# Comparing against an index row that lies in PSUM: one operand moved in the gates' one-hot matrices

## The chip, the cores and the metric

The kernel runs on one core of one Trainium2 chip. The metric is the device time of one execution in microseconds (us), the median of several runs; less is better. PE is the engine of the matmuls, DVE the vector engine, ACT the engine of activations, POOL the third elementwise engine, and SP issues most of the DMAs. SBUF is the working memory; PSUM is the memory into which matmuls write, eight banks of 512 fp32 numbers in each of 128 partitions.

## What is computed

A network of three blocks over 256 tokens of width 1024. The change lies in the first block's last part, a mixture of 16384 experts of one neuron each (PEER). Every token picks 16 experts for each of 8 heads, by the 16 best of 16 x 16 sums of two top-16 lists over 128 keys each. An expert's number is `i1 * 128 + i2`, and its weight is a softmax over the 16 best scores.

```python
def peer_ffn(h, w_query, sub_keys1, sub_keys2, expert_u, expert_v):
    ...
    e_idx = (jnp.take_along_axis(i1, top_p // PEER_TOPK, axis=-1) * PEER_N_KEYS
             + jnp.take_along_axis(i2, top_p % PEER_TOPK, axis=-1))
    gate = jax.nn.softmax(top_s, axis=-1)
    ...
    def block(args):
        xc, ic, gc = args
        u = jnp.take(expert_u, ic, axis=0)
        act = jax.nn.gelu(jnp.einsum('cd,ced->ce', xc, u).astype(jnp.float32), approximate=False)
        vv = jnp.take(expert_v, ic, axis=0)
        return jnp.einsum('ce,ced->cd', (gc * act).astype(vv.dtype), vv)
```

## The kernel before

The kernel gathers nothing. It computes all 16384 experts for all 256 tokens and multiplies each by its gate, which is zero for those not picked. `peer` (line 1026) does this in three stages.

First the queries, their scores and the two top-16 lists; `gates(t)` (line 1120) leaves, for each token, 128 picks in `pick`: index 0 is the one key's number, index 1 the other's, index 2 the weight. A pick is a partition there, a token a column.

Second, a loop over 128 tiles of 128 experts. `products(j)` (line 1195) multiplies tile j of `peer_u` with the tokens: 24 matmuls of 128x128 by 128x256 (eight pieces of the width, each as three products of split numbers, lines 106 to 108) into one PSUM bank, and ACT applies GELU. `prepare(j + 3)` readies a later tile: four DMAs from SP (`fetch`, line 1176), a DVE transpose into `uT`, and two halves of splitting, ACT for `uh` and POOL for `ul`.

Beside this loop, `spread` (line 1142) builds the gates, in 64 steps of N = 4 tokens. For a token, a one-hot matrix `b` says which pick has which first key, and `g` the same for the second key, scaled by the weight; the product of both, a 128x128 matmul, sums the weights of the picks into a table of gates. The function `ones(t0)` (line 1144) makes the matrices of four tokens: two DVE comparisons over 128x512 (`is_equal` of the index row `i128`, repeated for each token, with `pick`, repeated along the row), then four ACT scalings. The profile names them `one`. Then come four products (line 1158, eight matmul records, since fp32 goes in two passes) into one PSUM bank. Where the activations of a tile of experts are there already, DVE multiplies them with the gates in place (`G<-G,g`); where not, ACT copies the gates (`G<-g`), and `products` multiplies later (`G<-y,G`). `G` is read and written there in strides of 1 KB.

Third, the gated activations are multiplied with `peer_v` (lines 1281 to 1307).

Order: `V`, `A` and `P` (line 1033) keep DVE, ACT and POOL instructions of this function in the order of the program. PE's order is set by the planner of the framework. `advance` (line 1220) says how many steps of `spread` go with each tile; `ones` of the next step is issued after the products of this one.

PSUM is one pool (line 39) with three tags: "g" of four banks, "o" of two, "y" of two. `psum` (line 60) takes one of "g"; `pw` (line 64) goes in a cycle of three calls, g, g, o, with `k.turn` as its counter for the whole kernel. Within the second stage, the products take "g", GELU's results "y", and the spread products whatever `pw` gives. After the loop, line 1275 takes both "o" and both "y".

Of the kernel before, what the change touches and what calls it, by code (L numbers as in the profile page):

```python
# [11 lines left out]
F = mybir.dt.float32  # L12
# [1013 lines left out]
def peer(k, then):  # L1026


    nc, a, tc = k.nc, k.a, k.tc
# [3 lines left out]
    V, A, P = (Ordered(tc, e) for e in (nc.vector, nc.scalar, nc.gpsimd))  # L1033
    with ExitStack() as es:
# [8 lines left out]
        gap(k, part, GAPS["query"])  # L1043
        e1 = ExitStack()
        pool = e1.enter_context(tc.tile_pool(reuse_waits="tile", name="pu", bufs=1, side="right"))
        i128 = pool.tile([128, 128], F, name="i128")
        nc.gpsimd.iota(i128, pattern=[[1, 128]], base=0, channel_multiplier=0, allow_small_or_imprecise_dtypes=True)

        ph, pl = (pool.tile([128, 8, T], FR, name=x) for x in ("ph", "pl"))
        pick = pool.tile([128, 3, T], F, name="pick")  # L1050
# [6 lines left out]
        for i, nm in enumerate(("peer_sub_keys1", "peer_sub_keys2")):  # L1057
            skn = arena.tile([128, 128], F, name="skn", bufs=2)
            nc.scalar.dma_start(skn, a[nm][0])
            p = k.psum([128, 128])  # L1060
# [79 lines left out]
        N = 4  # L1140

        def spread(pool, first):

            def ones(t0):
                b, g = (pool.tile([128, N, 128], F, name=f"one{i}", bufs=2) for i in range(2))
                for o, i in ((b, 0), (g, 1)):
                    V.tensor_tensor(o, i128[:, None, :].to_broadcast([128, N, 128]),
                                    pick[:, i, t0:t0 + N, None].to_broadcast([128, N, 128]), op=OP.is_equal)
                for t in range(N):
                    A.activation(g[:, t], g[:, t], AF.Copy, scale=pick[:, 2, t0 + t:t0 + t + 1])  # L1150
                return b, g
            nxt = ones(0)
            yield 1
            for t0 in range(0, T, N):
                b, g = nxt
                p = k.pw([128, N, 128])
                for t in range(N):
                    nc.tensor.matmul(p[:, t], g[:, t], b[:, t], start=True, stop=True)
                if t0 + N < T:
                    nxt = ones(t0 + N)  # L1160
                n = state["done"]
                for x, at in ((G[0], 0), (G[1], NA)):
                    x = x[:, :, t0:t0 + N].rearrange("p j t -> p t j")
                    to = at + x.shape[2]
                    c = min(max(n, at), to)
                    if c > at:
                        V.tensor_tensor(x[:, :, :c - at], x[:, :, :c - at], p[:, :, at:c], op=OP.mult)
                    if c < to:
                        A.activation(x[:, :, c - at:], p[:, :, c:to], AF.Copy)
                state["built"] = t0 + N  # L1170
                yield (NB - 3 - first) * N / T
# [91 lines left out]
        for j in range(NB):  # L1263
            if not side and not state["built"]:
                e2.close()
                ow = e2.enter_context(tc.tile_pool(reuse_waits="tile", name="po", bufs=1, side="right"))
                side.append(spread(ow, j))
                pace = 1
            products(j)
# [4 lines left out]
        pool = es.enter_context(tc.tile_pool(reuse_waits="tile", name="pv", bufs=1))  # L1274
# [24 lines left out]
        for i in range(NB):  # L1299
# [3 lines left out]
            for c in range(8):  # L1303
                o, s = yp[c // 2][:, c % 2], slice(c * 128, c * 128 + 128)
# [734 lines left out]
@with_exitstack  # L2039
def program(ctx, tc, a, out, dbg=None, parts=None):  # L2040
    k = K(ctx, tc, a, out, dbg)
    first_half(k)
    norm = lambda l, j: lambda: Norm(k, k.of_norm(l, j), by4=l == j == 1)
    peer(k, norm(0, 0))
    with tc.tile_pool(reuse_waits="tile", name="ev", bufs=1) as pool:
        E = Even(pool)
        k.beside = even_weights(k, E, pool, 0)
        ffn(k, 0, 0, norm(0, 1))
        for _ in k.beside:
            pass  # L2050
        even_mixer(k, 0, E, norm(0, 2))
    with tc.tile_pool(reuse_waits="tile", name="s5", bufs=1) as ps5:
        S = S5(ps5)
        with tc.tile_pool(reuse_waits="tile", name="s5t", bufs=1) as tmp:
            k.beside = (None for _ in s5_weights(k, S, tmp, 0) for _ in range(2))
            ffn(k, 0, 1, norm(1, 0))
            ffn(k, 1, 0, norm(1, 1))
            for _ in k.beside:
                pass
        odd_mixer(k, 1, S, norm(1, 2))  # L2060
    ffn(k, 1, 1, lambda: Last(k))
    k.norm.done()
# [47 lines left out]
```

## Time and profile before

| | us |
|---|---|
| timed runs, median of 3 | 2390.65 |
| lowest and highest | 2383.12, 2391.75 |
| the profiled execution | 2374.76 |
| its span, first to last instruction | 2372.7 |
| PE busy | 2219.6 (94%) |
| DVE busy | 1801.2 (76%) |
| ACT busy | 1275.3 (54%) |
| POOL busy | 853.1 (36%) |
| mean granted TensorE clock | 0.964 |

The busy shares are means over stages with different limits. PE's busy time counts matmuls that overlap, so 94% isn't PE at its peak. [...] The profile names an instruction by what it writes and reads (`one<-i,pick` writes a `one` from `i128` and `pick`), leaving out the numbers of buffers. Lines 1001 are those of a helper, through which all DVE, ACT and POOL instructions of `peer` that keep their order are issued.

### The profile page before, as it was taken

Reading aid. Unit: us, or ns where it says so; the run is one execution under the profiler, and the core shown is the slowest. Engines: PE = TensorE matmul, PEld = TensorE weight load, DVE = VectorE, ACT = ScalarE, POOL = GpSimd, SP = SyncE. Lnnn points to the kernel's source line nnn. Section 1 sums busy time; section 2 is a strip of 40 time slices with the busy share of each in tenths; the row PEclk is TensorE's granted clock in tenths of the full one; section 3 lists DMA queues with packets and bytes.
Section 4 is the critical chain, followed back from the end, with each engine's and each line's share of the span. In section 5 each row is a group of like instructions: output and inputs, shape, how many; then the busy total and the mean of one; then the engine's idle time right before and its main releaser. Section 6 shows DMA issues by size and latency. Waiting matters only on the chain.

```text
span 2372.7 us, 46823 instructions
## 1 busy us (share of the span) xinstructions
PE 2219.6 (94%) x17962; PEld 2096.6 (88%) x17962; DVE 1801.2 (76%) x3277; ACT 1275.3 (54%) x2691; POOL 853.1 (36%) x829
## 2 busy tenths in 40 slices
PE   7999998788799999899999999999999999989998
PEld 4877687788799998899999899987999999979998
DVE  7888786898778999677777666667876666687664
ACT  4543433734478776455555554446656666536444
POOL 2132220678778787444444200100352221141000
PEclk8999798899999999999999999999999999989999
DMA  7522123446555554455555576521655455515663
GB/s 263 160 90 81 45 72 96 121 116 152 152 133 144 136 149 123 148 194 195 196 196 196 169 224 192 166 81 46 192 181 186 153 178 186 187 50 169 204 202 119
DMA packets 299232, 358.38 MB, mean 151 GB/s; under 512 B 19324, under 2 KB 271680, under 8 KB 297984
## 3 DMA queue, kind: packets, MB, share of 16 engines
q1 hardware_dynamic: 290432, 349.52, 47.6%
q10 hardware_dynamic: 8032, 5.54, 0.8%
q8 instruction: 141, 2.31, 0.4%
q14 instruction: 83, 0.68, 0.1%
q0 software_dynamic: 544, 0.33, 0.1%
HBM read 354.28 MB, written 1.05 MB: 150 GB/s over the span
## 4 chain that ended last, share of the span: by engine, by line
PE 64%; DVE 18%; DMA 6%; issue 4%; ACT 3%; POOL 3%; SPq 2%; DVEq 0%; ACTq 0%; POOLq 0%
PE g L106 8%; PE g L108 8%; PE g L107 8%; DMA u<-in_peer_u_dram 4%; DVE uT L1001 4%; PE o L106 3%; PE o L107 3%; PE o L108 3%; PE o L1305 2%; PE o L1306 2%; PE o L1307 2%; PE y L1306 2%; PE y L1305 2%; PE y L1307 2%; DVE one L1001 2%
## 5 line engine op out<-in xcount | busy, mean ns | idle before, releaser
L100 DVE TENSOR_TENSOR wl<-raw,wh 128x1024 fp32r<-128x1024 f32 (+3 forms) x381 | 431.9, 1136 | 216.4 <-ACT wh L99 205.5
L99 ACT ACTIVATE wh<-raw 128x1024 fp32r<-128x1024 f32 (+3 forms) x397 | 386.9, 977 | 385.0 <-PE g L107 180.0
L108 PE MATMUL g<-xh,wl 128*128 128x256 f32 x1864 | 524.8, 282 | 9.6 <-DVE wl L100 9.5
L106 PE MATMUL g<-xh,wh 128*128 128x256 f32 x1864 | 528.4, 284 | 4.9 <-ACT xh L374 2.5
L107 PE MATMUL g<-xl,wh 128*128 128x256 f32 x1864 | 523.8, 281 | 5.3 <-DVE xl L375 2.7
L1001 POOL TENSOR_TENSOR ul<-uT,uh 128x512 fp32r<-128x512 f32 x256 | 362.3, 1438 | 107.9 <-ACT uh L1001 102.1
L108 PEld LDWEIGHTS g<-xh,wl 128*128 128x128 f32 x1864 | 355.3, 191 | 13.4 <-DVE wl L100 12.6
L106 PEld LDWEIGHTS g<-xh,wh 128*128 128x128 f32 x1864 | 356.4, 192 | 11.2 <-issue 3.5
L107 PEld LDWEIGHTS g<-xl,wh 128*128 128x128 f32 x1864 | 355.0, 191 | 7.5 <-DVE xl L375 3.6
L108 PE MATMUL g<-ph,ul 128*128 128x256 f32 x1024 | 292.7, 286 | 16.8 <-POOL ul L1001 16.7
L106 PE MATMUL g<-ph,uh 128*128 128x256 f32 x1024 | 294.4, 288 | 6.8 <-ACT uh L1001 6.8
L107 PE MATMUL g<-pl,uh 128*128 128x256 f32 x1024 | 290.1, 283 | 0.0
L1292 POOL TENSOR_TENSOR vl<-v,vh 128x512 fp32r<-128x512 f32 x128 | 167.2, 1307 | 189.2 <-ACT vh L1291 187.5
L1291 ACT ACTIVATE vh<-v 128x512 fp32r<-128x512 f32 x256 | 147.8, 625 | 162.2 <-POOL vl L1292 69.2
L108 PEld LDWEIGHTS g<-ph,ul 128*128 128x128 f32 x1024 | 196.3, 192 | 22.0 <-POOL ul L1001 21.8
L106 PEld LDWEIGHTS g<-ph,uh 128*128 128x128 f32 x1024 | 196.4, 192 | 8.3 <-ACT uh L1001 8.2
L1001 ACT ACTIVATE uh<-uT 128x512 fp32r<-128x512 f32 x256 | 147.2, 624 | 99.1 <-DVE uT L1001 98.2
L106 PE MATMUL o<-hh,wh 128*128 128x256 f32 x704 | 196.8, 280 | 1.6 <-DVE t L1363 1.6
L107 PE MATMUL o<-hl,wh 128*128 128x256 f32 x704 | 196.4, 279 | 0.0
L107 PEld LDWEIGHTS g<-pl,uh 128*128 128x128 f32 x1024 | 196.3, 192 | 0.0
L108 PE MATMUL o<-hh,wl 128*128 128x256 f32 x704 | 196.1, 279 | 0.0
L126 DVE TENSOR_TENSOR al<-G,ah 128x256 fp32r<-128x256 f32 x128 | 171.5, 1341 | 16.2
(776 smaller groups left out, 5637.6 us busy)
## 6 DMA issues: line engine op xcount, KB each, us to landing
u<-in_peer_u_dram SPq DMA_DIRECT2D x512, 128.0 KB, 3.0
v<-in_peer_v_dram SPq DMA_DIRECT2D x64, 1024.0 KB, 4.9
raw<-in_ffn_w_gate_dram SPq DMA_DIRECT2D x44, 1024.0 KB, 5.8
raw<-in_ffn_w_up_dram SPq DMA_DIRECT2D x44, 1024.0 KB, 5.4
raw<-in_ffn_w_down_dram SPq DMA_DIRECT2D x32, 1024.0 KB, 5.3
raw<-in_ada_w_dram SPq DMA_DIRECT2D x24, 1024.0 KB, 5.3
raw<-in_w_in_dram SPq DMA_DIRECT2D x13, 1024.0 KB, 5.6
raw<-in_ffn_w_down_dram SPq DMA_DIRECT2D x16, 768.0 KB, 4.5
```

Source lines behind the costliest of these rows:

```text
L99: nc.scalar.activation(h, v, AF.Copy)
L100: self.sub.tensor_tensor(l, v, h.bitcast(F), op=OP.subtract)
L106: nc.tensor.matmul(out, sh, mh, start=first, stop=False)
L107: nc.tensor.matmul(out, sh, ml, start=False, stop=False)
L108: nc.tensor.matmul(out, sl, mh, start=False, stop=last)
L126: self.nc.vector.tensor_sub(l, src, h.bitcast(F))
L1001: return lambda *args, **kw: self.tc.keep_in_program_order(f(*args, **kw))
L1291: nc.scalar.activation(vh[:, s], r[:, s], AF.Copy)
L1292: eng.tensor_tensor(vl[:, s], r[:, s], vh[:, s].bitcast(F), op=OP.subtract)
L1305: nc.tensor.matmul(o, vh[:, s], ah, start=i == 0 and c % 2 == 0, stop=False, skip_group_check=True)
L1306: nc.tensor.matmul(o, vh[:, s], al, start=False, stop=False, skip_group_check=True)
L1307: nc.tensor.matmul(o, vl[:, s], ah, start=False, stop=i == NB - 1, skip_group_check=True)
```

## The change

The row of indices 0 to 127 is made in SBUF as before, under the name `i128s`. At its start, `spread` takes a bank of the tag "o" and copies the row there with one DVE instruction; `ones` compares with that copy. Since the bank is held for as long as `spread` runs, the spread products now take the tag "g" only, by `psum` in place of `pw`.

```diff
-        i128 = pool.tile([128, 128], F, name="i128")
-        nc.gpsimd.iota(i128, pattern=[[1, 128]], base=0, channel_multiplier=0, allow_small_or_imprecise_dtypes=True)
+        i128s = pool.tile([128, 128], F, name="i128")
+        nc.gpsimd.iota(i128s, pattern=[[1, 128]], base=0, channel_multiplier=0, allow_small_or_imprecise_dtypes=True)
...
         def spread(pool, first):
 
+
+            i128 = k.psum([128, 128], tag="o", bufs=2)
+            V.tensor_copy(i128, i128s)
+
             def ones(t0):
...
                 b, g = nxt
-                p = k.pw([128, N, 128])
+                p = k.psum([128, N, 128])
                 for t in range(N):
                     nc.tensor.matmul(p[:, t], g[:, t], b[:, t], start=True, stop=True)
```

## Rows read from the trace of the kernel before

**Rows 1.** The head of the profile page.
```profile
span 2372.7 us, 46823 instructions
```

**Rows 2.** By stretch: busy us (count) of PE, PEld, DVE, ACT, POOL; clock, DMA.
```profile
540.00:580.00 40.00, 35.23 (x290) 33.80 (x291) 33.65 (x87) 18.83 (x39) 31.83 (x26) 1.00 0.61 153
...
700.00:750.00 50.00, 49.80 (x426) 49.33 (x425) 41.51 (x63) 41.45 (x126) 40.74 (x29) 1.00 0.57 147
750.00:800.00 50.00, 47.83 (x409) 47.21 (x408) 47.83 (x65) 36.50 (x107) 39.77 (x27) 1.00 0.55 139
...
647.00:963.00 316.00, 295.84 (x2462) 292.00 (x2463) 290.69 (x396) 226.87 (x667) 242.98 (x164) 0.98 0.53 135
```

**Rows 3.** Waits, 640 to 965: who for whom, us in total, times, longest.
```profile
ACT one L1001 <- DVE one L1001: 63.7, 64, 2.3
...
PE g L1158 <- ACT one L1001: 21.1, 17, 5.0
...
DVE uT L1001 <- DMA u<-in_peer_u_dram: 12.6, 13, 2.0
```

**Rows 4.** Groups by shape, 647 to 963: busy us and mean ns, then idle before.
```profile
L1001 DVE TENSOR_TENSOR one<-i,pick 128x512 f32<-128x512 f32 x128 | 126.0, 1024 | 0.0
...
L1001 DVE TENSOR_TENSOR G<-G,g 128x288 f32<-128x288 f32 x28 | 23.0, 820 | 0.0
...
L1001 POOL TENSOR_TENSOR ul<-uT,uh 128x512 fp32r<-128x512 f32 x164 | 244.2, 1512 | 73.0 <-ACT uh L1001 67.4 <-PE o L1158 3.7 <-PE g L1158 1.9
```

**Rows 5.** Tile views: ns least/median/most, first and last start; `ul` before the spread.
```profile
L1001 DVE TENSOR_TENSOR one<-i,pick x128: 660/698/1815, 647.6 to 957.9; 128x512 f32<-128x512 f32 x128
...
L1001 DVE STREAM_TRANSPOSE uT<-u x84: 1211/1235/1253, 640.7 to 960.8; 128x1024 f32<-128x1024 f32 x84
...
L1001 DVE TENSOR_TENSOR G<-y,G x84: 152/276/425, 657.7 to 971.7; 128x256 f32<-128x256 f32 x3, 128x8 f32<-128x8 f32 x2, 128x20 f32<-128x20 f32 x2, 128x36 f32<-128x36 f32 x2
...
L1001 POOL TENSOR_TENSOR ul<-uT,uh x87: 1267/1289/1482, 486.7 to 639.7; 128x512 fp32r<-128x512 f32 x87
```

**Rows 6.** Timeline: start, us, instruction; in brackets its engine's idle time before.
```profile
657.79 1.28 DVE L1001 TENSOR_TENSOR one<-i,pick 128x512 f32<-128x512 f32 x2
...
658.56 2.93 POOL L1001 TENSOR_TENSOR ul<-uT,uh 128x512 fp32r<-128x512 f32 x2 [7.17 <-ACT uh L1001]
...
800.36 2.49 DVE L1001 TENSOR_TENSOR one<-i,pick 128x512 f32<-128x512 f32 x2
...
800.99 3.00 POOL L1001 TENSOR_TENSOR ul<-uT,uh 128x512 fp32r<-128x512 f32 x2 [0.36 <-ACT uh L1001]
...
803.39 1.37 PE L1158 MATMUL g<-one,one 128*128 128x128 f32 x8 [1.45 <-ACT one L1001]
```

**Rows 7.** Timeline of PE at the first, second and last gap of 17.
```profile
650.75 2.08 PE L1158 MATMUL g<-one,one 128*128 128x128 f32 x8 [4.99 <-ACT one L1001]
...
681.73 1.37 PE L1158 MATMUL g<-one,one 128*128 128x128 f32 x8 [0.23 <-ACT one L1001]
...
960.20 1.93 PE L1158 MATMUL g<-one,one 128*128 128x128 f32 x8 [2.63 <-ACT one L1001]
```

**Rows 8.** The same by stretch, behind two gaps; the clock is third from the end.
```profile
906.00:910.00 4.00, 4.00 (x21) 4.00 (x22) 4.00 (x6) 2.45 (x8) 2.16 (x3) 0.58 0.28 81
...
960.20:964.00 3.80, 3.80 (x18) 3.80 (x19) 3.37 (x6) 2.66 (x9) 3.07 (x4) 0.55 0.02 4
```

**Rows 9.** Groups by shape on DVE, whole kernel: copies out of PSUM.
```profile
L1437 DVE COPY wsT<-g 128x512 f32<-128x512 f32 x2 | 1.4, 692 | 0.3 <-PE g L1436 0.3
...
L293 DVE COPY V<-g 128x128 f32<-128x128 f32 x3 | 0.9, 289 | 4.5 <-PE g L291 4.4
```

**Rows 10.** Timeline: a spread product's first matmul and the last read of its bank.
```profile
800.89 1.05 PE L1158 MATMUL o<-one,one 128*128 128x128 f32 x8
...
804.12 0.46 ACT L1001 ACTIVATE G<-o 128x176 f32<-128x176 f32 x1
```

**Rows 11.** Waits of PE in the mixer of the second block, 1530 to 1725.
```profile
PE o L1623 <- DVE tq L1600: 3.2, 2, 2.7
```

## Prediction, made before the changed kernel had run

> **What bounds the kernel now.** I began with the span [rows 1], then asked for engine busy time by stretch around the code that changes. The spread (the stretch in which `spread` runs beside `products`) lasts from 647 to 963 us, 316 of the 2372.7 us. In it PE is busy 295.8 us, DVE 290.7, POOL 243.0 and ACT 226.9, at a granted clock of 0.98 [rows 2]. So two engines are close to full at once, PE and DVE. In some parts PE has no idle time (700 to 750: 49.8 of 50 us), in others DVE is the fuller one (750 to 800: 47.83 of 50, PE 47.83 too, and there PE does lose 2.2 us) [rows 2].
>
> The waits of that stretch say what stops PE: only one thing, `one` scaled by ACT, 17 times, 21.1 us, the longest 5.0. ACT in turn waits before every one of its 64 groups of scalings for DVE's `one`, 63.7 us in all [rows 3]. The chain of blame is therefore DVE `one`, ACT `one`, PE spread product.
>
> Next question: is DVE's `one` slow because it is long, or because something holds it? The group view gives 1024 ns as the mean of 128 instructions of one shape [rows 4]. The tile view gives 660/698/1815 for least, median and most [rows 5]. One shape with two durations 1.1 us apart is an instruction that is sometimes held. The timeline shows by whom: at 657.79, with POOL idle until 658.56, two `one` take 1.28 us. At 800.36, with POOL starting `ul` at 800.99, two take 2.49 [rows 6]. POOL suffers as well: its `ul` takes 1289 ns (median) before the spread begins and 1512 (mean) in it [rows 4, 5]. The other DVE instructions of the stretch run beside the same POOL work without this: the transpose `uT` (one SBUF input) 1211 to 1253 ns, and the product `G<-y,G` (one input in PSUM, one in SBUF) never above 425 ns at up to 256 elements [rows 5]. What sets `one` apart is that both of its inputs, `i128` and `pick`, are in SBUF.
>
> [...]
>
> **The change part by part.**
>
> *The copy into PSUM.* One DVE instruction, once, in front of the first `one`. A copy of 128x128 out of PSUM costs 289 ns [rows 9]; none into PSUM is in this trace, so I bound it by 0.1 and 0.6 us and take 0.29. It stands on the path, since PE is waiting at that point [rows 7].
>
> *The 128 comparisons.* `i128` now comes from PSUM. Does that make the instruction itself dearer? The nearest row is a DVE copy of 512 elements out of PSUM, 692 ns [rows 9]. The free `one` takes 660 to 698. I take 690. The ends: 660, and 1460 if PSUM cost what the `G` products cost per element (820 ns for 288 elements, 2.85 ns each [rows 4]); those step through SBUF in strides of 1 KB, the `y` products don't, and `one` doesn't, so I stay near the low end. DVE then has 128 x (1024 - 690) = 43 us less to do, POOL 164 x (1512 - 1289) = 37 us less.
>
> [...]
>
> What of this is on the path? Not 43 us, only what PE waits.
> - The first gap, 4.99 us at 650.75 [rows 7]. Two `one`, the first of them held, then one scaling. Priced by the held pair of rows 6 they fall from 2.49 to 1.28, and the copy adds 0.29: -0.9.
> - The other sixteen, 21.1 - 5.0 = 16.1 us, from 0.23 us at 681.73 to 2.63 at 960.20 [rows 3, 7]. At 803.39 the gap is 1.45 us; the pair in front of it is 2.49 - 1.28 = 1.21 us late through the hold alone [rows 6]. At that share (0.83) the sixteen lose 13.4. If the queue in front of the pair shrinks too, as 43 us less DVE work says, all 16.1 go. I take 14.5.
> - The clock. After the two longest gaps of the later spread the granted clock is 0.58 in 906 to 910 and 0.55 in 960.2 to 964, 1.2 GHz, the lower of the two levels, for about 3.4 us each [rows 8]; at half speed each costs 1.7 us. Without the gaps they should go: -3.4, bound 0. The drop behind the first gap stays, since that gap does.
> - What is late next: the u loads. DVE waits for them 12.6 us in 13 places now without PE being stopped by it [rows 3]. Before the spread, where they and the top-16 work set the pace, 290 matmuls in 40 us are 12.1 products, 3.31 us each [rows 2]. The spread has 82 products (two `ul` each [rows 4]), now 3.85 us each, and 3.6 after; they stay covered. I set aside 1.5 us for small waits of this sort.
>
> *Spread products in tag "g" only.* Before, every third had a bank of "o"; now 64 spread products and 82 products share four banks, 146 takings, 36 rounds, one in 8.2 us when the stretch takes 299 us. A spread product holds its bank from 800.89 to 804.58, 3.7 us, until ACT's copy of `G` has ended [rows 10]; a product holds it for its own 3.6 us and its GELU. No PE wait on a bank stands in the waits [rows 3]. So I cost it at nothing; the cover is the 3 to 4 us that a round is longer than a holding.
>
> *A side effect.* `pw` counts its calls in `k.turn`. The 64 calls of `spread` vanish from the count, and 64 is one more than a multiple of three, so in the attention and the two mixers behind, each call takes another place in the cycle of g, g, o. The waits there of the largest kind, PE for `o`, are 3.2 us in two places [rows 11]. I cost it at 0, with 4 us either way.
>
> **The sum.** -0.9 - 14.5 - 3.4 + 1.5 = -17.3 us. The next stage's loads and matmuls follow the spread's end, so it carries to the end of the span. The profiled execution took 2374.76 us (span 2372.7 [rows 1] and 2.1 around it), giving 2357.5. That execution lies 15.9 us under the median of the timed runs, 2390.65; the same difference from there gives 2373, my forecast for a median. Ends of this case: -12 (sixteen gaps at 13.4, no clock, 1.5 set aside, a dearer comparison) to -25 (all gaps, the clock, 4 us behind).
>
> **The rivals.**
> 1. *The pair is late through the queue, not through the hold.* The gap at 960.20 is 2.63 us, more than twice a hold of 1.21; DVE would still have about 248 us of work in 299. If only half of the gaps close, and the long ones, with their clock drops, stay: -0.9 - 8 + 1.5 = -7, so 2383. For it: DVE has hardly any idle time in 750 to 800. Against: the queue itself is full of holds.
> 2. *It doesn't do what it says*: an instruction with an input in PSUM is held all the same. Then only the copy is left: +0.3, 2391. Against it: `G<-y,G` never over 425 ns [rows 5].
> 3. *The four banks* (slower). Place: the first matmul of a product or a spread product, which waits until the bank of four takings ago is read out. It decides once a holding exceeds 8.2 us; each us beyond costs 36 us over 36 rounds. At 9.2 us, gain and loss give +19, so 2409. Against: 3.7 us of holding.
> 4. *A slow PSUM read* (slower). 1460 ns a comparison is 128 x 436 ns = 56 us more DVE work; DVE has 25 us idle in the stretch, so +31 and 2421. Against: the row of 692 ns.
>
> **How the numbers follow.** Chances: forecast 0.60, rival 1 0.22, rival 2 0.06, rival 3 0.08, rival 4 0.04. About 0.5% (12 us) is what a measurement of this kernel can tell from no change. Faster by more than that: the forecast, 0.60. Within: rivals 1 and 2, 0.28. Slower: 0.12. The range runs from the far end of the forecast (-25, and 5 us for the scatter of the runs, 2383 to 2392 before) to rival 2: 2360 to 2391. Rivals 3 and 4 stay out. The forecast's own range is 2361 to 2379.
>
> **What would show it.** In the profile after: `one` at 650 to 720 ns with no second cluster near 1780, and `ul` back at about 1290; the PE wait for ACT `one` down from 21.1 to 5 to 8 us, most of it at the first gap; DVE in the spread under 255 us; no low clock level near 906 and 960. A new line "PE waits for ACT or DVE `G`" would be rival 3. Gaps that stay behind short `one` would be rival 1. Wrong altogether if the time moves by more than 10 us outside 647 to 963.

## The result: 1.3% faster, about twice the forecast gain

The changed kernel takes 2352.82 us in the median of 4 runs (2344.87 to 2366.15); the kernel before took 2386.89 beside it (2382.05 to 2391.75). The ratio is 0.9868, with a 95% interval of 0.9828 to 0.9907: by this ratio 31 us less, between 22 and 41; the two medians lie 34 us apart. The profiled execution took 2351.32 us.

The head of the page of the changed kernel, as [rows 1]:

```profile
span 2349.4 us, 46836 instructions
```

Its waits in 635 to 965 us and, below, those of PE in 640 to 945 (us in total, times, longest), as [rows 3]:

```profile
DVE G L1001 <- ACT y L1001: 26.6, 42, 2.3
...
ACT one L1001 <- DVE one L1001: 19.9, 63, 0.4
DVE uT L1001 <- DMA u<-in_peer_u_dram: 19.8, 22, 2.2
...
PE g L1162 <- ACT one L1001: 3.9, 2, 3.6
PE g L108 <- POOL ul L1001: 0.6, 1, 0.6
```

PE's waits for `one` went from 21.1 us to 3.9, of which 3.6 is the first gap. ACT still waits for DVE's `one` before nearly each of its groups, but 0.3 us each and not 1.0. No wait of PE on a bank has come.

The groups by shape of the changed kernel in 652 to 945, as [rows 4], and the tile view of `one`, as [rows 5]:

```profile
L1001 DVE TENSOR_TENSOR one<-o,pick 128x512 f32<-128x512 f32 x128 | 81.7, 681 | 0.0
...
L1001 POOL TENSOR_TENSOR ul<-uT,uh 128x512 fp32r<-128x512 f32 x165 | 210.4, 1298 | 78.6 <-ACT uh L1001 77.7 <-PE g L1162 0.9
```
```profile
L1001 DVE TENSOR_TENSOR one<-o,pick x128: 661/681/708, 652.3 to 933.6; 128x512 f32<-128x512 f32 x128
```

The second cluster of `one` near 1780 ns is gone; the longest of 128 takes 708. (In the kernel before, counted one by one in the trace, 41 of the 128 lasted over 1 us and 65 under 700 ns; the prediction reckons with their mean, 1024 ns.) POOL's `ul` is back at its price outside the spread: 1298 ns in the mean, and 1289 (median) there [rows 5].

To compare the stretch itself I take it from the first `one` to the first load of `peer_v`, which every trace shows. First the changed kernel (us, then busy us and counts of PE, PEld, DVE, ACT, POOL, clock, DMA share, GB/s), as [rows 2]:

```profile
700.00:750.00 50.00, 50.00 (x443) 50.00 (x443) 41.27 (x65) 42.83 (x129) 36.61 (x30) 1.00 0.56 149
750.00:800.00 50.00, 50.00 (x443) 50.00 (x442) 44.28 (x75) 41.20 (x117) 37.65 (x30) 1.00 0.61 157
...
652.30:944.60 292.30, 290.15 (x2528) 289.75 (x2528) 249.17 (x397) 230.86 (x671) 209.48 (x167) 0.99 0.56 145
```

The same stretch of the kernel before, in its first trace and in a second one (the run r_before):

```profile
647.60:971.30 323.70, 304.06 (x2528) 300.02 (x2528) 291.50 (x398) 228.04 (x671) 244.73 (x167) 0.98 0.52 131
```
```profile
650.10:976.40 326.30, 305.36 (x2528) 301.03 (x2528) 295.18 (x398) 228.31 (x671) 245.70 (x167) 0.98 0.51 130
```

323.7 to 292.3: 31.4 us less, as much as the ratio of the timed runs says. The two spans differ by 23.3 only, since this execution took 4.7 us more ahead of the stretch and 3.4 us more behind it. PE's 2528 matmul records are the same work in all three lines. Its idle time (stretch less busy) falls from 19.6 us to 2.2, and its busy time falls too, by 13.9. The forecast had no term for most of the latter.

### The profile page after: what moved, and what is told of

Same layout as the page of the kernel before. It is cut to its first block, busy times and chain, and to the rows that moved or that the text cites. A ratio compares the mean times of both kernels' runs of the same rounds, so it can differ in the third digit from the quotient of the medians.

```text
span 2349.4 us, 46836 instructions
## 1 busy us (share of the span) xinstructions
PE 2207.7 (94%) x17962; PEld 2089.6 (89%) x17962; DVE 1761.5 (75%) x3277; ACT 1279.7 (54%) x2692; POOL 818.7 (35%) x829
## 3 DMA queue, kind: packets, MB, share of 16 engines
HBM read 354.28 MB, written 1.05 MB: 151 GB/s over the span
## 4 chain that ended last, share of the span: by engine, by line
PE 74%; DVE 14%; DMA 4%; issue 3%; POOL 3%; ACT 2%; SPq 1%; DVEq 0%; POOLq 0%; ACTq 0%
PE g L106 11%; PE g L108 11%; PE g L107 11%; PE o L106 3%; PE o L107 3%; PE o L108 3%; PE o L1309 2%; PE o L1311 2%; PE o L1310 2%; PE y L1309 2%; PE y L1311 2%; PE y L1310 2%; DVE uT L1001 2%; DMA u<-in_peer_u_dram 2%; PE g L1162 2%
## 5 line engine op out<-in xcount | busy, mean ns | idle before, releaser
L1001 POOL TENSOR_TENSOR ul<-uT,uh 128x512 fp32r<-128x512 f32 x256 | 327.4, 1302 | 113.9 <-ACT uh L1001 112.8
L106 PE MATMUL g<-ph,uh 128*128 128x256 f32 x1024 | 292.0, 285 | 6.8 <-ACT uh L1001 6.8
```

What stands on the lines that cost most here:

```text
L106: nc.tensor.matmul(out, sh, mh, start=first, stop=False)
L1001: return lambda *args, **kw: self.tc.keep_in_program_order(f(*args, **kw))
```

## The experiments

Times are given as a ratio to the kernel before, run beside them on the same chip, with a 95% interval; "the stretch" is the one above.

**Which part of the change does it? The tag alone (e1_tag_only, r_tag).**

```diff
-                p = k.pw([128, N, 128])
+                p = k.psum([128, N, 128])
```

> The index row stays in SBUF; only the banks change: the 64 spread products take tag g alone and no longer advance the counter of pw. Theory (the gain comes from the comparisons, which are no longer held by POOL's ul): no gain, 0 to +6 us against the kernel before; one keeps its two durations (660 and about 1780 ns), mean near 1024, and the stretch from the first one to the first load of v stays at 324 us within 5. Rival (the gain comes from the tag, by another order of PE and other places in the cycle of the later stages): most of the 34 us, -20 to -35 us, with one as slow as before.

Measured: 0.9996 (0.9978 to 1.0013), no gain. The tile view of `one` in the second trace (r_tag), and the stretch in the first:

```profile
L1001 DVE TENSOR_TENSOR one<-i,pick x128: 650/718/1819, 649.5 to 958.7; 128x512 f32<-128x512 f32 x128
```
```profile
648.90:967.80 318.90, 300.56 (x2528) 295.42 (x2528) 290.84 (x398) 227.37 (x671) 244.42 (x167) 0.99 0.52 133
```

The comparisons are as slow as before, and so is the kernel. The rival that the banks or the order of PE make the gain is out. The stretch is 5 to 7 us shorter than in both traces of the kernel before, so a second trace of it was taken.

> The tag alone once more, for a second trace: in the first the stretch was 5 to 7 us shorter than in the two traces of the kernel before, with no low clock late in it and no PE gap over 1.5 us, while the timed runs showed no gain. If that comes from the order of PE's work it stays (317 to 320 us, low clock 3 us); if it was chance the stretch is 322 to 327 us.

The stretch in that trace:

```profile
649.40:970.70 321.30, 300.94 (x2528) 295.22 (x2528) 293.98 (x398) 227.41 (x671) 244.94 (x167) 0.99 0.51 132
```

321.3 lies between the two expectations; the clock is 0.99 again, where both traces of the kernel before have 0.98. So the tag seems to shorten the stretch by some 2 to 7 us, through less time at the low clock. The timed runs don't show it, though their interval reaches to 5 us less; the part behind the stretch took 1401 to 1425 us in fourteen traces with no order in it that I can see, and hides such a difference in a single execution.

**The row alone (e2_row_only).** The changed kernel with the line of the tag put back:

```diff
-                p = k.psum([128, N, 128])
+                p = k.pw([128, N, 128])
```

> The index row in PSUM, the spread products still by pw (every third one in the bank of tag o that is left). Theory: the gain of the change stays whole, -25 to -38 us, one at 681 ns median with a most under 730, the stretch at 292 us within 4. A single o bank is taken again only after three products, some 10 us, and is held about 4, so no PE wait on a bank is expected. Rival (the tag makes the gain): 0 within 6 us though one is short. Third possibility (the tag costs something and the row gains more): a larger gain than with both, -38 to -45 us.

Measured: 0.9897 (0.9862 to 0.9932), 25 us less than before, at the near end of what was expected. Its stretch, and the one wait that is new in it:

```profile
645.30:942.40 297.10, 293.80 (x2528) 292.58 (x2528) 248.06 (x397) 231.13 (x671) 208.80 (x167) 0.99 0.55 143
```
```profile
DVE G L1001 <- PE o L1162: 13.0, 10, 2.2
```

The row makes the gain. The stretch is 5 us longer than with both parts, which I had not expected, and DVE waits 13.0 us for spread products in "o", a wait that the changed kernel doesn't show. The single bank that is left isn't short: its last product had been read out 8.7 us or more before each next one began. These products come late in PE's order: they start 2.9 us (mean of 21) after the first of their matrices is scaled, those in "g" 1.4 us (mean of 43), and PE is at products of the loop meanwhile. In the kernel before, with two "o" banks for them, the same means are 2.2 and 0.9. So the wait comes from PE's order, which the planner sets, and not from a want of banks. How it costs 5 us isn't shown: PE's idle time is 1.1 us longer, its busy time 3.7. In the timed runs the two intervals overlap; this 5 us rests on traces.

**Is it the row, or two operands in SBUF? (e3_pick).** The row stays in SBUF and the other operand moves:

```diff
+            two = k.psum([128, 2, T], tag="o", bufs=2)
+            V.tensor_copy(two, pick[:, 0:2])
...
-                                    pick[:, i, t0:t0 + N, None].to_broadcast([128, N, 128]), op=OP.is_equal)
+                                    two[:, i, t0:t0 + N, None].to_broadcast([128, N, 128]), op=OP.is_equal)
...
-                p = k.pw([128, N, 128])
+                p = k.psum([128, N, 128])
```

> The other operand moves: the index row stays in SBUF, and the two rows of indices in pick (128 x 512) are copied into the bank of tag o once; spread products in tag g. Theory (a comparison is held when both inputs are in SBUF, whichever one is moved): one at 680 ns median, most under 730, ul at 1300, the stretch at 292 us within 4, -25 to -40 us against the kernel before. Rival (something of the index row itself, its repetition or its place, made the comparisons slow): one keeps two durations, 0 within 6 us.

```profile
L1001 DVE TENSOR_TENSOR one<-i,o x128: 657/678/726, 654.1 to 935.7; 128x512 f32<-128x512 f32 x128
```
```profile
654.10:946.70 292.60, 290.72 (x2528) 290.52 (x2528) 249.00 (x397) 230.55 (x671) 209.31 (x166) 0.99 0.56 145
```

Measured: 0.9853 (0.9822 to 0.9884), the same gain. Either operand will do, and POOL is as free as in the changed kernel: busy for 209.3 us of the stretch, against 209.5 there and 244.7 in the kernel before. In these runs, then, a comparison with both inputs in SBUF is held beside POOL's `ul` (up to 1815 ns in the kernel before), and one with either input in PSUM is not (708 ns at most with the row there, 726 with `pick`). What it is in `ul` that takes part isn't shown; no run varies POOL's instruction.

**Is it DVE's lateness, or POOL's too? (e4_third, e8_half).** The changed kernel with one comparison of each step, or of every second step, made twice into the same matrix. That gives DVE its lost time back, 64 x 681 ns = 43.6 us or 21.8, without holding POOL.

```diff
-                for o, i in ((b, 0), (g, 1)):
+                for o, i in ((b, 0), (b, 0), (g, 1)):
```
```diff
-                for o, i in ((b, 0), (g, 1)):
+                for o, i in ((b, 0), (b, 0), (g, 1))[t0 // N % 2:]:
```

> The changed kernel with the first of the two comparisons of each step made twice into the same matrix: 64 more DVE instructions of 681 ns, 43.6 us, as much as the holds took from DVE, but with one input in PSUM, so POOL isn't held by them. Theory A (PE loses because DVE delivers one late, from whatever cause): the time goes back to that of the kernel before, -5 to +8 us, PE waits for one come back to 15 to 25 us, and DVE is over 95% busy again in 100 to 150 us of the stretch; ul stays at 1300 ns. Theory B (the two engines' holding each other makes the gain, POOL's part included): with ul at 1300 ns half of the gain or more stays, -15 to -30 us.

> As the run with 64 extra comparisons, but in every second step only: 32 more DVE instructions of 681 ns, 21.8 us, again free of holds. The 64 extra ones lengthened the stretch by 25.5 us against the changed kernel. If PE's loss is proportional to DVE's work, it is 13 us now (stretch 305 us, -19 us against the kernel before). If DVE first uses up its idle time (43 us of 292 in the changed kernel) and PE loses only beyond that, the stretch is 293 to 298 us, -25 to -32 us.

Measured: 0.9973 (0.9950 to 0.9995) with 64, and 0.9930 (0.9901 to 0.9960) with 32. The stretch with 64, then with 32, then without (the changed kernel again, r_after2):

```profile
650.80:968.00 317.20, 302.45 (x2528) 296.21 (x2528) 290.63 (x461) 226.58 (x670) 207.83 (x167) 0.99 0.53 134
```
```profile
651.70:954.00 302.30, 295.02 (x2528) 292.35 (x2528) 269.58 (x429) 228.69 (x671) 208.28 (x166) 0.99 0.55 140
```
```profile
650.30:942.30 292.00, 289.74 (x2528) 289.15 (x2528) 249.51 (x397) 230.88 (x671) 209.01 (x166) 0.99 0.55 145
```

(The first of these lines ends 0.4 us before the load of `peer_v` at 968.4; up to there the stretch is 317.6 us, PE busy for 302.7.) With DVE's 43.6 us back, some 25 of the gain's 31 us in the stretch are gone although POOL is as fast as in the changed kernel (207.8 us). So DVE's lateness is most of it; the time, 6 us under the kernel before, is just past the near end of theory A (-5) and far from theory B. What POOL's relief adds is seen beside the tag alone, which has as much DVE work and a held POOL: 317.6 us against 318.9 and 321.3 in the stretch, 0.9973 against 0.9996 in time, some 1 to 5 us; the intervals overlap, so this part isn't settled. The half dose lies between my two expectations in the stretch, 10.3 us, nearer to the proportional 13. The second half costs 15 us there, which would mean that DVE time gets dearer as DVE fills up; but by the timed ratios the first half costs 14 us and the second 10, so that isn't shown.

These three lines have the same clock and the same work, and there the missing term stands by itself. From no extra comparison to 64, PE's idle time grows by 12.6 us (2.3 to 14.9) and its busy time by 13.0 (289.7 to 302.7). Half of what PE loses when DVE has more to do is never idle time in the profile. The timeline of the run with 64 shows one way:

```profile
883.85 1.05 PE L1162 MATMUL g<-one,one 128*128 128x128 f32 x8
...
888.78 1.37 PE L1162 MATMUL g<-one,one 128*128 128x128 f32 x8 [1.15 <-ACT one L1001]
```
```profile
888.33 1.28 ACT L1001 ACTIVATE one<-one,pick 128x128 f32<-128x128 f32 x4 [1.07 <-DVE one L1001]
```

A group whose matrices are ready takes 1.05 us. One that waited takes 1.37, because its four tokens come at the pace of ACT's four scalings, 0.3 us each; the waiting inside stands as busy PE. In the kernel before it is the same at 803.39 [rows 6].

**The counter of pw (e5_turn).** The changed kernel with `k.turn += T // N` behind the copy.

> The changed kernel with the counter of pw advanced by 64 once, so that the later stages take their banks in the same places of the cycle as before the change. Theory (the counter matters little, the difference behind the stretch is scatter between executions): within 5 us of the changed kernel, -27 to -37 us against the kernel before. Rival (the shifted counter costs the later mixers 4 to 8 us, and hides part of the gain): -36 to -42 us.

Measured: 0.9867 (0.9833 to 0.9901), the changed kernel's own ratio, 32 us less than before, in the theory's range. The interval, 24 to 40 us, still takes in the near end of the rival, so nothing speaks for a cost of the counter, but a small one isn't shut out.

**The changed kernel again (r_after, r_after2), and the kernel before again (r_before).**

> The changed kernel once more, on the chip of these runs: -25 to -40 us against the kernel before, and a second trace of it, to see how much of the difference behind the stretch (+3.4 us in the first pair of traces) and ahead of it (+4.7 us) comes back. If it is scatter it changes its size or sign; if it is the counter of pw it stays at +2 to +5 us behind the stretch.

> The changed kernel beside the version whose spread begins later, on one chip: -28 to -36 us against the kernel before, stretch 291 to 293 us, one PE gap of 3.6 to 4.3 us at its beginning.

> The kernel before once more, for a second trace: the stretch at 317 to 324 us, one in two durations. The part behind it took 1401 us in the first trace and 1405 to 1419 in all others; if that was scatter it is 1405 to 1415 now. Low clock in the stretch 3 to 13 us; if it is 3 as in the run with the tag alone, the two late drops of the first trace (3.4 us of time in all) were not a fixed part of the cost.

Measured: 0.9872 (0.9842 to 0.9903) and 0.9871 (0.9837 to 0.9905). The stretch took 291.7 and 292.0 us, the part behind it 1409 and 1421. The kernel before, a second time, took 326.3 and 1405. The gain is steady and lies in the stretch; ahead of it and behind it executions scatter. The low clock of the first trace came back in the second, with mean clock 0.98.

**A version that goes further (e6_later, r_later).** The gap at the beginning is left; PE comes to the first spread product before its matrices exist. Here the first step asks for more products of the loop first:

```diff
             nxt = ones(0)
-            yield 1
+            yield 2.5
```

> The changed kernel with the first step of spread asking for 2.5 products instead of 1 before its first product, so that the first four matrices are ready when PE comes to them. Theory: the one gap that is left (3.6 to 4.2 us), and the 3.4 us of low clock behind it, go: 4 to 6 us less than the changed kernel, -35 to -40 us against the kernel before. Rival (the planner moves the spread product ahead again, or the gates then end later than the loop): no gain over the changed kernel within 3 us.

> The version whose spread begins later once more: by its first trace, which has neither the gap nor the low clock behind it, 4 to 6 us under the changed kernel of the same call. If the median is not lower by at least 2 us, the gain is not to be told from none by these runs.

```profile
PE g L1162 <- ACT one L1001: 0.5, 2, 0.3
```
```profile
645.20:700.00 54.80, 54.58 (x479) 54.38 (x478) 44.19 (x69) 47.27 (x137) 42.52 (x35) 1.00 0.64 163
...
750.00:932.00 182.00, 181.70 (x1589) 181.11 (x1588) 164.21 (x264) 139.85 (x406) 130.18 (x104) 1.00 0.54 143
```

Measured: 0.9846 (0.9814 to 0.9879) and 0.9849 (0.9815 to 0.9882); beside r_after2 the medians are 2349.85 and 2356.04. The gap is gone, and with it the low clock in the stretch (1.00 throughout); PE is idle for less than 1 us of 288. From the 1001st matmul of the loop to its last, the same work in every version, it is 296.0 and 296.1 us in its two traces and 300.6 to 301.0 in three of the changed kernel. Both ratios are lower by 0.002, but the intervals overlap with the changed kernel's: a gain of about 5 us that is seen in the traces and not settled by the times.

## Why the prediction was wrong in size

The forecast was 2373, with a range down to 2360; the measured 2352.8 lies below it. Of the 20.5 us between, 14.1 are the gain in the stretch (17.3 forecast, 31.4 measured), the rest is in the medians: that of the kernel before was 3.8 us lower beside this run than the one I started from, and the two lie 2.7 us further apart than the stretches. The mechanism was the one forecast, and each of the rivals is out: no comparison is held and none takes 1460 ns (708 at most), no gap over 0.6 us but the first is left and PE waits on no bank. Of the signs named, PE's wait for `one` fell further than the 5 to 8 us, to 3.9. The sign of 10 us outside the stretch was too fine: the part behind it alone scatters by 24 over all traces.

- **The comparison, the copy, POOL.** 690 ns was forecast and 681 measured; 0.29 us and 0.27; `ul` 1289 and 1298; 43 us of DVE time and 42.3 (291.5 to 249.2 in the stretch). A dearer comparison, for which the forecast's near end left room, doesn't show: 681 with a PSUM input, 660 to 698 for the free ones without. The copy and the first gap, in the timeline of the changed kernel:

```profile
651.96 0.27 DVE L1001 COPY o<-i 128x128 f32<-128x128 f32 x1
652.26 2.48 DVE L1001 TENSOR_TENSOR one<-o,pick 128x512 f32<-128x512 f32 x4
...
654.04 1.94 PE L1162 MATMUL g<-one,one 128*128 128x128 f32 x8 [3.59 <-ACT one L1001]
```

- **The gaps.** First one: -0.9 forecast, -1.4 measured (4.99 to 3.59). The other sixteen: -14.5 forecast, -15.8 measured (16.1 to 0.3). In the stretch's own lines idle time falls by 17.5. Right, and my doubt about the queue in front of the pair wasn't needed.
- **The clock.** -3.4 forecast, for the two late drops, which are gone. The drop behind the first gap became shorter as well, which I had left at 0. The granted clock, a share of full speed, has two values in the traces of both kernels, 1.00 and 0.50. In the kernel before, matmuls of 256 columns that follow each other start every 113 ns at the first and every 213 at the second (652.84 to 656.47); 256 columns in 213 ns are 1.2 per ns, which is what the traces show for the prediction's 1.2 GHz. Here is the kernel before, then the changed one, behind that gap:

```profile
650.70:654.00 3.30, 3.25 (x15) 3.25 (x16) 2.97 (x4) 2.30 (x9) 0.69 (x1) 0.50 0.06 10
654.00:658.00 4.00, 4.00 (x26) 4.00 (x26) 0.84 (x3) 0.99 (x5) 0.00 (x0) 0.66 0.51 132
```
```profile
654.00:658.00 4.00, 3.96 (x20) 3.96 (x21) 2.43 (x4) 2.84 (x9) 1.27 (x2) 0.57 0.29 78
```

  At half speed a share of 0.50 over 3.3 us and 0.66 over 4.0 is 6.0 us of low clock, 0.57 over 4.0 is 3.4; half of the difference, 1.3 us, is gained. Together -4.7. The tag alone does as much: there PE waits as long in all as before, but behind the first gap in pieces of 1.4 us at most, and in both of its traces 3.4 us of low clock are all that is left.
- **What is late next.** +1.5 set aside, 0 measured. DVE does wait longer for the u loads (12.6 to 19.8 us), since it has the time; PE doesn't feel it.
- **The step that failed** is "only what PE waits". I read PE's loss off the waits, 21.1 us, which is idle time between records. PE's busy time fell by 13.9 us for the same 2528 records; 4.7 of that is the clock, and 9.2 stood in no term of mine. It is seen without the clock in the tag alone (300.6 and 300.9 us busy at 0.99) against the changed kernel (289.7 to 290.2 at 0.99), and once more with the extra comparisons. Some 6 us of it are the spread groups that go at ACT's pace: at the same clock they are busy for 81.1 us with the tag alone (r_tag) and for 75.2 in the changed kernel, by the groups by shape of PE:

```profile
L1158 PE MATMUL g<-one,one 128*128 128x128 f32 x512 | 81.1, 289 | 22.6 <-ACT one L1001 22.4
```
```profile
L1162 PE MATMUL g<-one,one 128*128 128x128 f32 x512 | 75.2, 277 | 3.9 <-ACT one L1001 3.9
```

  The rest can be counted from the start of one PE record to the start of the next, in the traces of r_tag and of r_after2, where PE is busy for 11.2 us less. Inside the spread groups the steps shrink by 5.8 us. From a product's record to the spread record behind it, 118 times in either, 43.0 us become 20.7, while the idle time shown there falls from 20.2 to 2.1: 4.1 us more are lost than are shown as idle. PE's records overlap: one of 128x256 lasts 0.28 us, but in a full stretch one comes every 0.113 (443 in 50 us). By these two numbers, an estimate, a gap can be shown up to 0.17 us too short, and PE waits 27 times in r_tag. The last 1.3 us lie between records of products, which come every 117 instead of every 113 ns in parts of r_tag; why is open. The run with 64 extra comparisons parts its 13.0 us in the same way: 5.2, 4.6 and 3.0.

With -17.5 for idle time and -13.9 for busy time, the sum is the measured -31.4. The page before had the sign already: in 750 to 800 there were 409 records in 47.83 busy us, 117 ns each, where 113 is what the changed kernel needs [rows 2]. Even 700 to 750, which the prediction read as a part without idle time, holds 426 records, where the changed kernel has 443.

- **The tag** cost nothing, as said, and the four banks never ran short; that the spread products in "o" come later in PE's order, and that without them DVE is spared a wait, I hadn't seen. **The counter** of `pw` moves nothing that these runs can measure.

## What to carry to other kernels

If DVE compares two tensors in SBUF beside POOL work, look for two durations of one shape (here under 700 ns and up to 1815), and put either operand into PSUM where a bank is free (681 and 678 ns here). If PE is the engine that loses, don't price the loss by its idle time alone: take the records per busy us in a stretch where nothing is late, and count the slower ones as well. And when a change moves work to other banks, look where that work then stands in PE's order before you call the banks short.

## What the runs showed of the hardware that I had not expected

- A DVE comparison of 128x512 with one input in PSUM takes 681 ns, as with both in SBUF and free (660 to 698), for either of the operands (681 and 678).
- A PE that waits piece by piece is booked as busy: with 43.6 us of extra DVE work, 12.6 us of PE's loss was idle and 13.0 busy, 5.2 of the latter inside the spread groups.
- The low clock is paid for twice late in the spread of the kernel before, in both of its traces. In the second, its two stretches at the low clock (0.50 and 0.51) are these:

```profile
911.30:914.70 3.40, 3.40 (x18) 3.40 (x18) 3.40 (x5) 2.05 (x7) 1.56 (x3) 0.50 0.27 82
965.80:969.20 3.40, 3.40 (x18) 3.40 (x17) 2.74 (x5) 2.02 (x7) 2.67 (x3) 0.51 0.02 5
```

  The longest PE wait late in the spread is 2.6 us in the first of those traces and 2.7 in the second. With the tag alone PE waits as much in all, but in smaller pieces, and from 665 to 966 its clock is 1.00 in both traces. PE's waits in that stretch (us in total, times, longest), from the two traces of the kernel before and then the two of the tag alone:

```profile
PE g L1158 <- ACT one L1001: 16.1, 16, 2.6
```
```profile
PE g L1158 <- ACT one L1001: 17.5, 19, 2.7
```
```profile
PE g L1158 <- ACT one L1001: 16.4, 24, 1.3
```
```profile
PE g L1158 <- ACT one L1001: 18.3, 26, 1.4
```
